# Two projections of the convolution branch computed by tokens in blocks of seven products, and the copies for the weight sums of w_out made earlier

## The chip, the cores and the metric

The kernel runs on one core of one Trainium2 chip. A time is the device time of one execution in microseconds (us); the time of a kernel is the median of its runs. The profile is of one more execution, and its times count from the first to the last instruction. In it PE is TensorE (matmuls; PEld is its weight load), DVE VectorE, ACT ScalarE, POOL GpSimd, SP the engine that issues most of the DMAs.

## The reference, cut to what matters

One layer over x of 256 tokens and 2048 channels, all in float32:

```python
hn = _rmsnorm(h, norm_w[i])
proj = hn @ w_in[i]                       # 2048 x 18432
q, v, f_fwd, f_bwd, z_a, b_gate, c_gate, h_b, z_b = jnp.split(proj, IN_SPLITS, axis=-1)
o_a = _hgrn2_bidirectional(jax.nn.silu(q), v, f_fwd, f_bwd, lb_all[:, i])
o_a = _head_rmsnorm(o_a, hgrn_norm_w[i]) * jax.nn.silu(z_a)
y_b = b_gate * _short_conv(c_gate * h_b, conv_w[i])      # width 3, per channel, along tokens
o_b = _rmsnorm(y_b, conv_norm_w[i]) * jax.nn.silu(z_b)
h = h + jnp.concatenate([o_a, o_b], axis=-1) @ w_out[i]  # 4096 x 2048
gate = jax.nn.sigmoid(h @ w_ple_gate[i])
h = h + (p[i] @ w_ple[i]) * gate
return _rmsnorm(h, final_norm_w)
```

Each of the nine groups of columns of w_in is 2048 wide. c_gate and h_b are needed only as their product, which the convolution then takes along the tokens, channel by channel.

## The kernel before, in words

**Products.** Every float32 value is split into a high and a low part; a float32 product is three matmuls (high by high, high by low, low by high). The weights come from HBM as blocks of 1 MB into `raw` (three buffers); `Stream` splits each half of a block (1024 columns) into `spl` (five buffers): ACT writes the high part (L121), DVE subtracts it for the low part (L122). Three splits are asked for ahead of use.

**Three ways to multiply.** `gemm_in` puts channels on the partitions: for a k-tile and 128 channels one 512-wide matmul (L427) and one 256-wide (L425); 32 such pairs make 256 channels of one projection, and `evac` adds the two parts (ACT L487, DVE L488). `gemm_vz` puts tokens on the partitions and takes v and z_a of two values of i at a time: `half` walks over eight blocks of two k-tiles, each as 24 products of 512 columns (3 per `three`, L547 to L549). A block named in `VZ_SUMS` takes seven block products in the place of eight, 21 instead of 24; for it `add_up` makes three sums of weights on DVE (L83), and the sums of x stand ready in `xq`. The result is scaled by the row norm afterwards. The output projection uses `half` too, with sums of mixa and mixb (L532 to L543) and sums of w_out that are prepared in DRAM: `prepare` copies 2 x 512 KB from DRAM to DRAM on SP's queue (L330), and `add_up` adds onto the copies by accumulating DMAs on POOL's queue (L338, L342).

**Stages.** Group A (`two_pairs`, i = 0, 2, 4, 6): q, forget gates, v and z_a, and the recurrence of two pairs of heads. Group B (loop at L924, i = 0 to 7, 256 channels each): c_gate, h_b, b_gate, z_b with `gemm_in`; the norm multiply of c_gate and the product with h_b on POOL; the convolution on DVE; y = convolution times b_gate on POOL; sigmoid of z_b on ACT; DVE's gate (L956), POOL's product (L960), and the split into mixb (ACT L973, DVE L974). In the same steps sums of mixa and mixb for the output are made. `pump` issues one of 48 accumulation steps after each POOL multiply and, after the last step of a sum, asks for the prepare of the fourth next one. Then come the output projection, the gate and the last norm.

**Order.** Functions write instructions; `at(dt, fn)` puts one off by dt ticks of the matmul loops; a priority scheduler sets the order on each engine, each of which runs its instructions in that order.

Of the kernel before, what the change touches and what calls it, by code (L numbers as in the profile page):

```python
# [8 lines left out]
F32 = mybir.dt.float32  # L9
# [128 lines left out]
def tile_hymba_encoder(  # L138
# [35 lines left out]
    VZ_ORDER, VZ_SUMS, VZ_OWN = range(8), (2, 4, 6), (2, 4, 6)  # L174
    dramp = ctx.enter_context(tc.tile_pool(name="dramp", bufs=1, space=bass.MemoryType.DRAM))
    vz_prepared = {}
    blocks = {}
    for i in range(0, 8, 2):
        for ii in (i, i + 1):
            for c in (B_FF, B_FB, B_Q):  # L180
                blocks[c, ii] = sum((ws.add(w_in[c + ii, h]) for h in range(2)), [])

        if i:
            blocks[B_V, i], vz_prepared[i] = [], []
            for q in VZ_ORDER:
                srcs = [
                    [w_in[c + i + b, q // 4, :, 2 * (q % 4) : 2 * (q % 4) + 2] for b in range(2)] for c in (B_V, B_ZA)
                ]
                if q in VZ_OWN:
                    blocks[B_V, i].append(ws.add_own(*srcs))  # L190
                elif q in VZ_SUMS:
                    sums = dramp.tile([P, 4, 512], F32, name=f"vz{i}_{q}")
                    vz_prepared[i].append((srcs, sums))
                    blocks[B_V, i].append(ws.add_sums(*srcs, sums))
                else:
                    blocks[B_V, i].append(ws.add(*srcs[0], *srcs[1]))
            continue
        for c in (B_V, B_ZA):
            blocks[c, i] = sum(
                (ws.add(*(w_in[c + i + b, q // 2, :, 4 * (q % 2) : 4 * (q % 2) + 4] for b in range(2))) for q in range(4)), []  # L200
            )
    for i in range(8):
        for c in (B_CG, B_HB, B_BG, B_ZB):
            blocks[c, i] = sum((ws.add(w_in[c + i, h]) for h in range(2)), [])
    first_out = len(ws.todo)
# [29 lines left out]
    rx, rb, rf, most, dummy = (few[:, 2 * j : 2 * j + 2] for j in range(5))  # L235
# [83 lines left out]
    now = [0]  # L319

    def at(dt, fn):
        pend.append((now[0] + dt, len(pend), fn))
# [69 lines left out]
    def x_norms():  # L392
        dve.tensor_reduce(out=rx, in_=ss8, op=ALU.add, axis=AX.X)
        act.activation(rx, rx, AF.Sqrt, bias=epst, scale=1.0 / D)
        dve.reciprocal(out=rx, in_=rx)
        for m in range(2):
            dve.tensor_copy(rw[m], rx[:, m : m + 1].broadcast_to([P, P]))
# [56 lines left out]
    xq = []  # L454

    def gemm_vz(i, vt, zt):

        acc = [psg.tile([P, 512], F32, tag="g", name=f"avz{i}_{b}") for b in range(4)]
        sc = [t.rearrange("p a b -> p (a b)") for t in scps]

        def extra():
            x, y = (psm.tile([P, 512], F32, tag=t, name=f"e{t}{i}") for t in "xy")
            return [x, y, *sc]

        main = [[acc[m], acc[2 + m]] for m in range(2)]
        for q1, q5, q6, q7 in half(main, extra, VZ_ORDER, VZ_SUMS, blocks[B_V, i], xs, xq[0], True):
            d = xq[1][:, 0]
            with tc.high_priority(offset=400):
                act.copy(out=vt[:, 0], in_=q1)
                dve.tensor_tensor(out=d, in0=vt[:, 0], in1=q6, op=ALU.subtract)  # L470
                dve.tensor_tensor(out=zt[:, 0], in0=q5, in1=d, op=ALU.subtract)
                dve.tensor_tensor(out=vt[:, 1], in0=d, in1=q7, op=ALU.subtract)
                dve.tensor_tensor(out=zt[:, 1], in0=zt[:, 0], in1=q7, op=ALU.add)
        with tc.high_priority(offset=400):
            for n, dst in enumerate((vt, zt)):
                for m in range(2):
                    dve.tensor_tensor(out=dst[:, m], in0=main[m][n], in1=dst[:, m], op=ALU.add)
            for dst in (vt, zt):
                for m in range(2):
                    act.activation(dst[:, m], dst[:, m], AF.Copy, scale=rx[:, m : m + 1])  # L480
# [36 lines left out]
    mixa = mixp.tile([P, NH * 2 * T + 8], F32R, name="mixa")[:, : NH * 2 * T]  # L517
    mixa = mixa.rearrange("p (k s t) -> p k s t", k=NH, s=2)
# [31 lines left out]

    def half(main, extra, order, which, parts, src, sums, every):
# [9 lines left out]
        for q, ids in zip(order, parts):  # L561
            k = 2 * q
            if len(ids) == 2:
                some_n = ((0,), (1,)) if every and q in (order[0], order[-1]) else ((0, 1),)
                for kk, n in ((kk, n) for ns in some_n for kk in range(2) for n in ns):
                    w = ws.get(ids[kk])[:, 0].rearrange("p s (b n) -> p b s n", b=2)
                    for m in range(2):
                        ah, al = (src[:, k + kk, s, m * P : (m + 1) * P] for s in range(2))
# [10 lines left out]
            def one(kk, m):  # L579
                return [src[:, k + kk, s, m * P : (m + 1) * P] for s in (1, 0)]  # L580

            def some(o):
                return [src[:, k, s, P:] if o == sums.shape[2] else sums[:, z, o, s] for s in (1, 0)]
# [228 lines left out]
    def two_pairs(i):  # L812
# [5 lines left out]
        if i == 6:  # L818
            for z in range(4):
                at(10 + 10 * z, lambda z=z: prepare(prepared[z]))  # L820
        else:


            todo = vz_prepared[i + 2]
            for z, what in enumerate(todo):
                at(50 + 10 * z, lambda what=what: prepare(what))
                for step in range(3):

                    dt = (166, 196, 220)[step] + z if i else 98 + 6 * step + z
                    at(dt, lambda what=what, step=step: add_up(what, step))  # L830
        if i == 2:

            def xsums(z):
                k = 2 * VZ_SUMS[z]
                a, t = xq[1][:, 0].rearrange("p (k t) -> p k t", k=2), xq[1][:, 1].rearrange("p (o t) -> p o t", o=4)
                act_sums(xs[:, k : k + 2], a, t, tc.keep_in_program_order)
                act_split(xq[0][:, z], xs[:, k : k + 2], t)
# [31 lines left out]
        if i == 0:  # L869
# [9 lines left out]
            xq.append(xqp.tile([P, len(VZ_SUMS), 4, 2, P], F32R, name="xsum"))  # L879
            xq.append(xqp.tile([P, 2, 512], F32, name="xd"))  # L880
# [10 lines left out]
        def rest():  # L891
# [5 lines left out]
            else:  # L897

                def keep():
                    kept.extend(psm.tile([P, 2, 2, P], F32, tag=f"sc{e}", name=f"kept{e}") for e in range(2))  # L900
                    finish_two(ogs, ss, zt, kept)
# [14 lines left out]
    mixb = None  # L916
# [6 lines left out]
    pool.memset(ysum, 0.0)  # L923
    for i in range(8):  # L924
        cg = ctmp.tile([P, 2, T], F32, tag="cg", name=f"cg{i}", bufs=2)
        evac(gemm_in(B_CG, i, TURNED if i % 2 == 0 else {}), lambda m: cg[:, m, :], ctmp)
        hb = ctmp.tile([P, 2, T], F32, tag="hb", name=f"hb{i}", bufs=2)
        evac(gemm_in(B_HB, i, {} if i else TURNED), lambda m: hb[:, m, :], ctmp)
        u = ub[i % 2]
        by_norms(cg, rbc2, 2)  # L930
        pump()
        pool.tensor_tensor(out=u[:, :, 1 : T + 1], in0=cg, in1=hb, op=ALU.mult)
        pump()
# [8 lines left out]
        evac(gemm_in(B_BG, i, {} if i else TURNED), lambda m: hb[:, m, :], ctmp)  # L942
# [6 lines left out]
        evac(gemm_in(B_ZB, i, TURNED if i in (0, 6) else {}), lambda m: hb[:, m, :], ctmp)  # L949
# [12 lines left out]
        if i == 0:  # L962
# [3 lines left out]
            mixb = bp.tile([P, NH, 2, T], F32R, name="mixb")  # L966
            og = bp.tile([P, 2, 2, 2, P], F32, name="og")
            suma = bp.tile([P, len(SUMS), 3, 2, P], F32R, name="suma")
        if i == 2:
            for e in range(2):  # L970
                act.copy(out=og[:, e], in_=kept[e])
        hi, lo = mixb[:, 2 * i : 2 * i + 2, 0, :], mixb[:, 2 * i : 2 * i + 2, 1, :]
        act.copy(out=hi, in_=cg)  # L973
        dve.tensor_tensor(out=lo, in0=cg, in1=hi, op=ALU.subtract)  # L974
        for src, z, n in ((mixa, i - 1, len(SUMS)), (mixb, i - SUMS[0], len(sumb32))):
            if 0 <= z < n:
                k = 2 * SUMS[z]
                a = ctmp.tile([P, 2, T], F32, tag="tmp", name=f"sa{i}")
                if src is mixb:
                    act_sums(mixb[:, k : k + 2], a, sumb32[z])  # L980
# [34 lines left out]
    tmp = spare.tile([P, 2, 512], F32, name="tmp")  # L1015
    tmps = [*(tmp[:, b] for b in range(2)), *(og[:, e].rearrange("p m h t -> p (m h t)") for e in range(2))]
# [46 lines left out]
    for u in range(2):  # L1063
# [9 lines left out]
        for src, sums, main, other, scale in ((mixa, suma, psg, psm, False), (mixb, sumb, psm, psg, True)):  # L1073
# [3 lines left out]
            if u == 0 and not scale:  # L1077
                for z in range(len(SUMS)):
                    k = 2 * SUMS[z]
                    if z == len(sumb32):  # L1080
                        sumb32.append(tmp[:, 0].rearrange("p (o t) -> p o t", o=4))
                        act_sums(mixb[:, k : k + 2], tmp[:, 1].rearrange("p (k t) -> p k t", k=2), sumb32[z])
                    act_split(sumb[:, z], mixb[:, k : k + 2], sumb32[z])
# [182 lines left out]
```

## Time and profile before

| | |
|---|---|
| median of 3 runs | 1111.88 us (1110.82 to 1114.4) |
| profiled execution | 1112.2 us |
| its span, first to last instruction | 1110.5 us |
| granted TensorE clock | 0.998 |
| group B | about 513 to 835 us of the span |
| v and z_a of a later pair in A | for example 195 to 239 us |

A row of a group reads: line, engine, operation, written tile <- read tiles, shape, count, busy time in all, mean ns of one, idle time before it and what ended that. A row of a timeline reads: start, duration, engine, line, and in brackets the idle time ahead of it and its releaser. Durations overlap where an engine works on instructions one behind the other.

### The profile page before, as it was taken

How to read it: one execution, taken by the hardware profiler on the slowest of the kernel's cores; microseconds unless marked ns; L12 is line 12 of the kernel's file. 1: busy time of each engine (PE TensorE's matmuls, PEld its weight loads, DVE VectorE, ACT ScalarE, POOL GpSimd, SP SyncE). 2: the span in 40 equal slices, each digit the busy share in tenths (PEclk: the TensorE clock that was granted, in tenths of full speed). 3: DMA queues.
4: the chain of work that ended last, by engine and by line, in shares of the span. 5: the costliest groups of instructions: out<-in, count | busy, mean ns of one | idle time of the engine just before them, and what ended most of it. 6: DMA issues, size and time to landing. Idle time of an engine off the chain costs nothing.

```text
span 1110.5 us, 16882 instructions
## 1 busy us (share of the span) xinstructions
PE 1100.5 (99%) x6455; PEld 945.7 (85%) x6455; DVE 851.4 (77%) x1127; ACT 677.3 (61%) x946; POOL 269.1 (24%) x215
## 2 busy tenths in 40 slices
PE   9999999999999999999999999999999999999997
PEld 8888888888888888888888888888888888888886
DVE  7799578896889778997657758856667888887673
ACT  6786577667876697575545535535546575575562
POOL 1045015203530325043334223424331000000101
PEclk9999999999999999999999999999999999999999
DMA  9755454564457744758999998999979887887542
GB/s 340 272 187 190 153 190 157 171 242 153 161 162 258 292 152 152 231 172 228 298 310 250 270 334 231 282 345 254 288 196 306 318 299 286 286 312 253 193 133 76
DMA packets 69808, 260.44 MB, mean 235 GB/s; under 512 B 7008, under 2 KB 16608, under 8 KB 52192
## 3 DMA queue, kind: packets, MB, share of 16 engines
q1 hardware_dynamic: 60480, 242.25, 62.1%
q0 software_dynamic: 8960, 16.78, 10.0%
q8 instruction: 51, 0.84, 0.3%
q10 hardware_dynamic: 288, 0.34, 0.1%
q14 instruction: 29, 0.24, 0.1%
HBM read 257.25 MB, written 35.65 MB: 264 GB/s over the span
## 4 chain that ended last, share of the span: by engine, by line
PE 98%; DMA 1%; ACT 0%; SPq 0%; DVE 0%; DVEq 0%; issue 0%; ACTq 0%
PE a L427 37%; PE a L425 19%; PE avz L547 3%; PE avz L548 3%; PE avz L549 3%; PE pg L1027 3%; PE pg L1026 3%; PE pg L1028 3%; PE pa L547 2%; PE pa L548 2%; PE pa L549 2%; PE a L446 1%; PE a L448 1%; PE a L447 1%; PE pb_sc L548 1%; PE pb_sc L549 1%
## 5 line engine op out<-in xcount | busy, mean ns | idle before, releaser
L122 DVE TENSOR_TENSOR spl<-raw,spl 128x1024 fp32r<-128x1024 f32 (+2 forms) x419 | 505.0, 1219 | 163.6 <-ACT spl L121 160.2
L427 PE MATMUL a<-xs,spl 128*128 128x512 f32 x1792 | 617.3, 395 | 0.6 <-ACT spl L121 0.6
L121 ACT CAST spl<-raw 128x1024 fp32r<-128x1024 f32 (+2 forms) x419 | 414.1, 999 | 255.0 <-PE a L425 81.9
L425 PE MATMUL a<-xs,spl 128*128 128x256 f32 x1792 | 483.8, 278 | 0.0
L427 PEld LDWEIGHTS a<-xs,spl 128*128 128x128 f32 x1792 | 332.2, 188 | 73.6 <-ACT spl L121 1.0
L425 PEld LDWEIGHTS a<-xs,spl 128*128 128x128 f32 x1792 | 334.6, 188 | 5.8 <-DVE spl L122 0.5
L1143 POOL TENSOR_TENSOR hh<-hh,fw 128x512 f32<-128x512 f32 (+1 forms) x9 | 11.0, 1227 | 250.7 <-ACT gt L1142 248.0
L487 ACT COPY r<-a 128x256 f32<-128x256 f32 x112 | 40.5, 368 | 37.3 <-PE a L425 35.8
L547 PE MATMUL avz<-spl,xs 128*128 128x512 f32 x138 | 54.0, 391 | 0.0
L549 PE MATMUL avz<-spl,xs 128*128 128x512 f32 x138 | 53.7, 389 | 0.0
L548 PE MATMUL avz<-spl,xs 128*128 128x512 f32 x138 | 53.7, 389 | 0.0
L1026 PE MATMUL pg<-spl,ht 128*128 128x512 f32 (+1 forms) x120 | 45.2, 377 | 0.0
L1027 PE MATMUL pg<-spl,ht 128*128 128x512 f32 (+1 forms) x120 | 45.1, 376 | 0.0
L1028 PE MATMUL pg<-spl,ht 128*128 128x512 f32 (+1 forms) x120 | 45.0, 375 | 0.0
L716 POOL TENSOR_TENSOR qc<-pf,ge 128x256 f32<-128x256 f32 x16 | 18.3, 1148 | 105.8 <-ACT dd L706 91.8
L492 POOL TENSOR_TENSOR xf<-xf,rbc 128x1024 f32<-128x1024 f32 x8 | 19.9, 2486 | 94.0 <-DVE rbc L403 50.2
L121 ACT CAST spl<-early 128x1024 fp32r<-128x1024 f32 (+1 forms) x29 | 28.7, 990 | 19.1 <-PE pb_y L549 7.5
L122 DVE TENSOR_TENSOR spl<-early,spl 128x1024 fp32r<-128x1024 f32 (+1 forms) x29 | 32.9, 1147 | 9.2 <-ACT spl L121 8.8
L547 PE MATMUL pa<-spl,mixa 128*128 128x512 f32 x88 | 34.5, 392 | 0.0
L549 PE MATMUL pa<-spl,mixa 128*128 128x512 f32 x88 | 34.3, 389 | 0.0
L548 PE MATMUL pa<-spl,mixa 128*128 128x512 f32 x88 | 34.2, 389 | 0.0
L716 POOL TENSOR_TENSOR kc<-dd,ge 128x256 f32<-128x256 f32 x16 | 27.7, 1728 | 19.8 <-DVE dd L707 13.6
(321 smaller groups left out, 1641.7 us busy)
## 6 DMA issues: line engine op xcount, KB each, us to landing
raw<-in_w_in_dram SPq DMA_DIRECT2D x106, 1024.0 KB, 6.9
raw<-in_w_in_dram SPq DMA_DIRECT2D x100, 256.0 KB, 3.9
raw<-in_w_out_dram SPq DMA_DIRECT2D x36, 512.0 KB, 5.2
sums<-in_w_out_dram SPq DMA_DIRECT2D x32, 512.0 KB, 10.6
raw<-in_w_in_dram SPq DMA_DIRECT2D x26, 512.0 KB, 5.2
raw<-sums SPq DMA_DIRECT2D x13, 1024.0 KB, 5.3
raw<-in_w_gate_dram SPq DMA_DIRECT2D x9, 1024.0 KB, 5.1
sums<-in_w_out_dram POOLq DMA_DIRECT2D x16, 512.0 KB, 10.1
```

Source lines behind the costliest of these rows:

```text
L121: self.nc.scalar.copy(out=v[:, :, 0], in_=r)
L122: self.nc.vector.tensor_tensor(out=v[:, :, 1], in0=r, in1=v[:, :, 0], op=ALU.subtract)
L425: pe.matmul(a[:, :T], lhsT=lhsT, rhs=xs[:, kt, 0, :], start=False, stop=(kt == NKT - 1))
L427: pe.matmul(a, lhsT=lhsT, rhs=xs[:, kt, :, :].rearrange("p s n -> p (s n)"), start=(kt == 0), stop=False)
L487: act.copy(out=r, in_=acc[m][:, 1, :])
L547: pe.matmul(acc, lhsT=ah, rhs=w[:, 0], start=start, stop=False)
L548: pe.matmul(acc, lhsT=ah, rhs=w[:, 1], start=False, stop=False)
L549: pe.matmul(acc, lhsT=al, rhs=w[:, 0], start=False, stop=stop)
L716: pool.tensor_tensor(out=c64(dst[:, d]), in0=c64(src[:, d, :, half * P : (half + 1) * P]), in1=g.unsqueeze(3).broadcast_to([P, 2, 2, CH]), ...
L1026: pe.matmul(acc[m], lhsT=lh, rhs=wh, start=(kt == 0), stop=False)
L1027: pe.matmul(acc[m], lhsT=lh, rhs=wl, start=False, stop=False)
L1028: pe.matmul(acc[m], lhsT=ll, rhs=wh, start=False, stop=(kt == nk - 1))
```

## The change

For i = 2, 4 and 6, c_gate and h_b of two values of i are computed together, tokens on the partitions, by `gemm_pair`, which is taken out of `gemm_vz`. Blocks 2 and 4 of eight are done as seven products. The results a and b become a * rx2 * b (rx2 is the square of the row norm) by two DVE instructions, are transposed by PE (eight 128x128 transposes) at 12 ticks into the b_gate projection, and ACT copies them to the convolution's input. POOL's norm multiply and product are gone for these i.

The sums of x for blocks 2 and 4 have to live through group B and move to the end of `mixa`; mixb becomes eight tiles, the last two of which share their place with a and b. The kept results of A go to another SBUF tile in the place of PSUM.

The prepares of w_out's sums are no longer asked for by `pump`: each of the four stages of A issues four of them. Four of the accumulation steps are asked for within each new stage.

```diff
-    for i in range(8):
+    CH_SUMS = (2, 4)
+    for i in range(2):
         for c in (B_CG, B_HB, B_BG, B_ZB):
             blocks[c, i] = sum((ws.add(w_in[c + i, h]) for h in range(2)), [])
+    for i in range(2, 8, 2):
+        blocks[B_CG, i] = []
+        for q in VZ_ORDER:
+            srcs = [
+                [w_in[c + i + b, q // 4, :, 2 * (q % 4) : 2 * (q % 4) + 2] for b in range(2)] for c in (B_CG, B_HB)
+            ]
+            blocks[B_CG, i].append(ws.add_own(*srcs) if q in CH_SUMS else ws.add(*srcs[0], *srcs[1]))
...
         if steps_up:
             n, step = steps_up.pop(0)
             add_up(prepared[n], step)
-            if step == 2 and n + 4 < len(prepared):
-                prepare(prepared[n + 4])
...
-        if i == 6:
-            for z in range(4):
-                at(10 + 10 * z, lambda z=z: prepare(prepared[z]))
...
+        for z in range(4):
+            at(10 + 22 * z, lambda z=z: prepare(prepared[2 * i + z]))
...
-            xq.append(xqp.tile([P, len(VZ_SUMS), 4, 2, P], F32R, name="xsum"))
-            xq.append(xqp.tile([P, 2, 512], F32, name="xd"))
+            xq.extend((late[:, 0], late[:, 1], xqp.tile([P, 4, 2, P], F32R, name="xsum")))
+            xd.append(xqp.tile([P, 2, 512], F32, name="xd"))
...
+    def convolved(i, ut):
+
+        for ii in (i, i + 1):
+            tp = psm.tile([P, 2, T], F32, tag="xy"[ii % 2], name=f"ut{ii}")
+            for h in range(2):
+                c = (2 * (ii % 2) + h) * P
+                for m in range(2):
+                    pe.transpose(tp[:, h, m * P : (m + 1) * P], ut[:, m, c : c + P], ident)
+            act.copy(out=ub[ii % 2][:, :, 1 : T + 1], in_=tp)
+
+    def gemm_ch(i):
+
+        def get():
+            a, b = (bp.tile([P, 2, 512], F32, tag=f"late{e}", name=f"ch{i}_{e}") for e in range(2))
+            return a, b, early[:, 0:512]
+
+        for z in range(4):
+            at(5 + 10 * z, pump)
+        a, b = gemm_pair(f"ch{i}", CH_SUMS, blocks[B_CG, i], get)
+        with tc.high_priority(offset=300):
+            for m in range(2):
+                dve.scalar_tensor_tensor(
+                    out=a[:, m], in0=a[:, m], scalar=rx2[:, m : m + 1], in1=b[:, m], op0=ALU.mult, op1=ALU.mult
+                )
+        at(12, lambda: convolved(i, a))
+
     for i in range(8):
...
-        evac(gemm_in(B_ZB, i, TURNED if i in (0, 6) else {}), lambda m: hb[:, m, :], ctmp)
+        hb = ctmp.tile([P, 2, T], F32, tag="hb", name=f"zb{i}", bufs=2)
+        evac(gemm_in(B_ZB, i, kick), lambda m: hb[:, m, :], ctmp, 500 if i in (1, 3, 5) else 200)
```

What `gemm_pair` does behind its products is what `gemm_vz` did; line numbers move by up to some 40 (L122 and L83 stay; L427 becomes L433, L425 L431, L488 L500, L956 L997, L960 L1001, L974 L1017, L532 L545, L535 L548).

On DVE, where the stage for i = 4 begins: the first seven-product block's weights are `raw_6323`; they get three sums (L83) and four splits (L122), among which the gate of i = 3 (L997), mixb's low part (L1017) and the sums of mixa and mixb (L545, L548) stand.

```order
669 L83 TENSOR_TENSOR raw_6323<-raw_6323 128x2x512
670 L997 SCALAR_TENSOR_TENSOR zb_6188<-zb_6188,vec,szb_6285 128x256
671 L545 TENSOR_TENSOR sa_6293<-mixa 128x512
672 L122 TENSOR_TENSOR spl_6350<-raw_6323,spl_6350 128x512
673 L1017 TENSOR_TENSOR mixb_5141<-cg_6175,mixb_5141 128x2x256
674 L83 TENSOR_TENSOR raw_6323<-raw_6323 128x512
675 L122 TENSOR_TENSOR spl_6365<-raw_6323,spl_6365 128x2x512
676 L83 TENSOR_TENSOR raw_6323<-raw_6323 128x512
677 L548 TENSOR_TENSOR sb_6294<-sa_6293 128x128 x2
678 L548 TENSOR_TENSOR sb_6294<-sa_6293,sb_6294 128x128 x2
679 L545 TENSOR_TENSOR sa_6304<-mixb_5141 128x512
680 L122 TENSOR_TENSOR spl_6386<-raw_6323,spl_6386 128x2x512
```

The same place before, where c_gate of i = 4 begins:

```order
660 L122 TENSOR_TENSOR spl_6362<-raw_6341,spl_6362 128x4x256
661 L956 SCALAR_TENSOR_TENSOR hb_6003<-hb_6003,vec,szb_6292 128x256 x2
662 L532 TENSOR_TENSOR sa_6302<-mixa 128x512
663 L535 TENSOR_TENSOR sb_6303<-sa_6302 128x128
664 L122 TENSOR_TENSOR spl_6383<-raw_6381,spl_6383 128x4x256
665 L974 TENSOR_TENSOR mixb<-cg_5914,mixb 128x2x256
666 L535 TENSOR_TENSOR sb_6303<-sa_6302 128x128
667 L535 TENSOR_TENSOR sb_6303<-sa_6302,sb_6303 128x128 x2
668 L532 TENSOR_TENSOR sa_6313<-mixb 128x512
669 L122 TENSOR_TENSOR spl_6411<-raw_6381,spl_6411 128x4x256
```

Behind the first gate row two splits stood before (664, 669); now three splits (672, 675, 680) and two sums of weights (674, 676) of one block stand there, with the third sum (669) right ahead, in line with the same gate and mix rows.

On POOL, from the gate product of i = 1 (L1001, before L960) to the product of the convolution and b_gate of i = 2 (L983, before L943), in the change:

```order
125 L1001 TENSOR_TENSOR cg_5146<-cg_5146,zb_5429 128x512
126 L349 DMA sums_0_5_84<-sums_0_5_84 128x512
127 L345 DMA sums_1_2_85<-in_w_out_dram 256x1x512
128 L345 DMA sums_1_3_86<-in_w_out_dram 256x1x512
129 L345 DMA sums_1_4_87<-in_w_out_dram 256x1x512
130 L345 DMA sums_1_5_88<-in_w_out_dram 256x1x512
131 L983 TENSOR_TENSOR cg_5955<-cg_5955,bg_5854 128x512
```

And before:

```order
125 L960 TENSOR_TENSOR cg_5116<-cg_5116,hb_5205 128x512
126 L342 DMA sums_0_5_84<-sums_0_5_84 128x512
127 L492 TENSOR_TENSOR cg_5515<-cg_5515,early 128x512
128 L338 DMA sums_1_2_85<-in_w_out_dram 256x1x512
129 L932 TENSOR_TENSOR ub_4596<-cg_5515,hb_5604 128x2x256
130 L338 DMA sums_1_3_86<-in_w_out_dram 256x1x512
131 L943 TENSOR_TENSOR cg_5515<-cg_5515,hb_5604 128x512
132 L338 DMA sums_1_4_87<-in_w_out_dram 256x1x512
```

The multiplies that stood between the accumulating copies are gone, so that four stand one behind the other.

More of the change, by code (lines that the diff above doesn't have):

```diff
@@ L201, in tile_hymba_encoder @@
             )
-    for i in range(8):
+    CH_SUMS = (2, 4)
+    for i in range(2):
         for c in (B_CG, B_HB, B_BG, B_ZB):
             blocks[c, i] = sum((ws.add(w_in[c + i, h]) for h in range(2)), [])
+    for i in range(2, 8, 2):
[6 more added lines that the diff above has]
+        for ii in (i, i + 1):
+            for c in (B_BG, B_ZB):
+                blocks[c, ii] = sum((ws.add(w_in[c + ii, h]) for h in range(2)), [])
     first_out = len(ws.todo)
@@ L234, in tile_hymba_encoder @@
     few = const.tile([P, 16], F32, name="few")
-    rx, rb, rf, most, dummy = (few[:, 2 * j : 2 * j + 2] for j in range(5))
+    rx, rb, rf, most, dummy, rx2 = (few[:, 2 * j : 2 * j + 2] for j in range(6))
     xf32 = xp.tile([P, NKT, T], F32, name="xf32")
@@ L395, in x_norms @@
         dve.reciprocal(out=rx, in_=rx)
+        dve.tensor_tensor(out=rx2, in0=rx, in1=rx, op=ALU.mult)
         for m in range(2):
@@ L477, in gemm_vz @@
                     dve.tensor_tensor(out=dst[:, m], in0=main[m][n], in1=dst[:, m], op=ALU.add)
+        return vt, zt
+    def gemm_vz(i, vt, zt):
+        gemm_pair(f"vz{i}", VZ_SUMS, blocks[B_V, i], lambda: (vt, zt, xd[0][:, 0]))
+        with tc.high_priority(offset=400):
             for dst in (vt, zt):
@@ L1072, in tile_hymba_encoder @@
             )
-        for src, sums, main, other, scale in ((mixa, suma, psg, psm, False), (mixb, sumb, psm, psg, True)):
+        for src, sums, main, other, scale in ((mixa, sums_a, psg, psm, False), (mixb, sums_b, psm, psg, True)):
             name = f"p{'ab'[scale]}{u}"
```

91 lines of the change are left out of this document (47 added, 44 removed).

## The prediction

> **What bounds the kernel now.** I read first the spans, then the chain of waits, then what TensorE (PE) waited for.
>
> ```profile
> span 1110.5 us, 16882 instructions
> PE 1100.5 (99%) x6455; PEld 945.7 (85%) x6455; DVE 851.4 (77%) x1127; ACT 677.3 (61%) x946; POOL 269.1 (24%) x215
> PE 98%; DMA 1%; ACT 0%; SPq 0%; DVE 0%; DVEq 0%; issue 0%; ACTq 0%
> core 0: 1110.5 us, clock 0.998
> PE wps L266 <- DVE wz L261: 1.1, 1, 1.1
> PE a L427 <- ACT spl L121: 0.6, 1, 0.6
> ```
>
> The chain is 98% matmuls, the granted clock is 0.998, and the last two rows are the whole list of PE's waits: 1.7 us, both at the start. So nothing but less matmul work makes this kernel shorter, and any weight split that comes late makes it longer at once. DVE, at 77%, has time over on average; whether it has in one stage must be asked there. The next rows are stretches of the span; their columns are the stretch, its length, busy time of PE, weight loads, DVE, ACT and POOL with counts, clock, DMA share and GB/s.
>
> ```profile
> 568.40:612.80 44.40, 44.40 (x258) 38.83 (x257) 28.83 (x40) 21.06 (x30) 17.82 (x12) 1.00 0.94 257
> 330.30:352.06 21.76, 21.76 (x98) 18.02 (x97) 19.44 (x21) 12.87 (x14) 0.00 (x0) 1.00 0.69 221
> 195.00:239.00 44.00, 44.00 (x273) 36.51 (x273) 40.20 (x45) 27.74 (x34) 5.63 (x4) 1.00 0.61 202
> 474.00:513.00 39.00, 39.00 (x313) 34.55 (x312) 34.84 (x43) 22.97 (x44) 16.72 (x13) 1.00 0.67 198
> 513.00:835.00 322.00, 322.00 (x1860) 281.59 (x1859) 216.84 (x293) 156.87 (x215) 109.38 (x89) 1.00 0.93 274
> 251.70:262.91 11.21, 11.21 (x66) 9.62 (x64) 8.45 (x10) 6.90 (x17) 5.58 (x5) 1.00 0.49 182
> ```
>
> The first is four projections with channels on the partitions in group B: 128 pairs of a 512-wide and a 256-wide matmul. The second is 96 token-major 512-wide products. The third is a whole v/z_a stage, where blocks of seven products are already in use: DVE has 40.20 of 44.00 us to do there and PE still lost nothing. The fifth is group B, with DMA at 0.93.
>
> **The change part by part.**
>
> *Matmuls.* Per pair of i (three pairs) four projections of 32 matmul pairs go. I price them at 44.39 us (11.09 each; the window's 44.40 less its cut edges). In their place come eight blocks, six of 24 products and two of 21: 186 products. From the second window one is 21.76 / 96 = 0.2267 us, so 42.17 us. Added are eight transposes per pair; their price stands in the chain, where eight of the same shape lie between two projection matmuls:
>
> ```profile
> 182.73 0.23 PE a L427
> 182.97 0.12 PE a L425
> 183.09 0.87 PE ogt L658 x8
> 183.96 0.23 PE a L427
> L658 PE MATMUL ogt<-ident,ogz x24: 270/272/273, 182.9 to 418.5; 128*128 128x128 f32 x24
> ```
>
> 0.87 us, and I add 0.09 for two groups of four going in separately, and 0.06 for the moved kicks of the weight order. Per pair 42.17 + 0.87 + 0.15 - 44.39 = -1.2; three pairs give **-3.6 us**. As PE waited for nothing in B, this is also the most that can be gained.
>
> The Trainium skill, "TensorE: Matmul & The Clock Gate", Part 4 (PE-mode transpose), gives some 275 ns for one 128x128 transpose inside a kernel, with the PE's access latency as its largest part. Twenty-four of them one behind the other would be an estimated 6.6 us and leave no gain. The last row above agrees with that figure as a duration (272 ns), but the chain row shows that the next one starts after 0.87 / 8 = 0.109 us, so the trace goes with the overlap.
>
> *DVE, in the new stage.* The elementwise cost is where a stall can come from. Rows from the same work in B now (start, duration, instruction):
>
> ```profile
> 600.21 2.35 DVE L122 TENSOR_TENSOR spl<-raw,spl 128x1024 fp32r<-128x1024 f32 x2
> 615.31 0.42 DVE L488 TENSOR_TENSOR hb<-a,r 128x256 f32<-128x256 f32 x1
> 618.17 0.87 DVE L956 SCALAR_TENSOR_TENSOR hb<-hb,vec,szb 128x256 f32<-128x256 f32 x2
> 619.08 0.69 DVE L532 TENSOR_TENSOR sa<-mixa 128x512 f32<-128x512 f32 x1
> 619.80 1.27 DVE L535 TENSOR_TENSOR sb<-sa 128x128 f32<-128x128 f32 x1
> 622.13 0.68 DVE L974 TENSOR_TENSOR mixb<-cg,mixb 128x512 fp32r<-128x512 f32 x1
> 617.20 0.63 ACT L953 ACTIVATE szb<-hb 128x512 f32<-128x512 f32 x1 [0.28 <-POOL hb L492]
> 620.96 0.62 ACT L973 CAST mixb<-cg 128x512 fp32r<-128x512 f32 x1 [1.27 <-POOL cg L960]
> 615.87 1.29 POOL L492 TENSOR_TENSOR hb<-hb,rbc 128x512 f32<-128x512 f32 x1 [6.44 <-DVE hb L488]
> 619.19 1.74 POOL L960 TENSOR_TENSOR cg<-cg,hb 128x512 f32<-128x512 f32 x1 [1.24 <-DVE hb L956]
> L83 DVE TENSOR_TENSOR raw<-raw 128x512 f32<-128x512 f32 x6 | 4.6, 763 | 0.2
> L83 DVE TENSOR_TENSOR raw<-raw 128x1024 f32<-128x1024 f32 x3 | 3.7, 1217 | 0.0
> L122 DVE TENSOR_TENSOR spl<-raw,spl 128x1024 fp32r<-128x1024 f32 x18 | 22.8, 1282 | 3.0 <-ACT spl L121 2.6
> ```
>
> Of two 1024-wide splits in a dense row the second starts 1.14 us after the first (2.35 for both, with the last one's tail); I take that for the 1024-wide weight sum too, and 0.6 for a 512-wide one, about half. The last three rows, of the third window's stage, are means of busy time, 1.28, 1.22 and 0.76: longer, since instructions behind one another overlap.
>
> The tight place is the first seven-product block. PE reaches its last summed weights after 48 products of blocks 0 and 1 and 21 of its own: 69 x 0.2267 = 15.64 us after the stage's start. In that time DVE has, by the order shown for the pair that starts at i = 4 (the excerpt has the last twelve rows): the evacuation of the projection before (0.84), three wide splits (3.42) and a narrow one (0.66), three weight sums (2.3), the two gates (0.86), two 512-wide sums of mixa and mixb (1.44), the four small ones (1.06), mixb's low part (0.68): 11.3 us. The rest is waiting: the sums of weights stand in line behind the gate L997, and this behind POOL's 1.29 and ACT's 0.63; the mixb rows stand behind POOL's 1.74 and ACT's 0.62; the evacuation ends only 1.7 us in. Walking these rows one by one, each starting when its releaser is done, the last split is ready 15.7 to 15.8 us after the start against 15.64. At i = 2, without the mixb sum, it is ready at 15.1 to 15.3, and at i = 6 earlier. So I put **+0.2 us** on the path, all at i = 4. The lower bound is 0, the upper, with the means of busy time in the place of the distances, 2.3 + 4.8 = 7.1 us. I take the low one: the v/z_a stage above works with these same blocks at 91% DVE and no wait.
>
> *POOL.* The norm multiply of c_gate and the product with h_b go from POOL for six of the eight i; it is at 24%, so this is worth nothing by itself. The result goes out by ACT's copy from PSUM instead; the next conv needs it during the b_gate projection, 11 us, and takes two copies of some 0.6 us. Nothing on PE waits there.
>
> *Copies of w_out.* Twelve pairs of copies move from B into the first three stages of A. They run beside PE; what they can delay is a raw load. Rows for the queues (share of all 16 engines) and for issue to landing:
>
> ```profile
> q1 hardware_dynamic: 60480, 242.25, 62.1%
> q0 software_dynamic: 8960, 16.78, 10.0%
> sums<-in_w_out_dram SPq DMA_DIRECT2D x32, 512.0 KB, 10.6
> raw<-in_w_in_dram SPq DMA_DIRECT2D x106, 1024.0 KB, 6.9
> 573.52 1.05 ACT L121 CAST spl<-raw 128x1024 fp32r<-128x1024 f32 x1 [4.81 <-DMA raw<-in_w_in_dram]
> ```
>
> In the last stage of A four such pairs already run, and the fourth window shows PE full there at a DMA share of 0.67. I take **0** for them, since 22 ticks apart they are spread wider than these; if that cover is gone, one late load at the stage with the narrowest lead would cost up to its 6.9 us less the 5.5 us that two splits cover, so 0 to +1.4. B loses the same bytes: its 0.93 falls, and the split that waited 4.81 us for a load (and cost PE nothing) has more room. Worth 0 too, as no PE wait stands behind it.
>
> **Sum.** The profiled execution took 1112.2 us, 0.3 above the median of 1111.88. 1112.2 - 3.6 + 0.2 = 1108.8 for a profiled one, **1108.5** for the median. A difference under 0.3% (3.3 us) can't be told from none in a measurement of this kernel; the forecast lies at that edge.
>
> **The rivals.**
>
> *A: DVE is late for the seven-product blocks.* Place: first sum block at i = 2 and 4. For it: DVE there has gate, mix sums and weight sums in one line in program order, and one late POOL multiply (rows of POOL in B reach far more than 1.74) moves the whole line:
>
> ```profile
> 576.31 2.14 POOL L492 TENSOR_TENSOR hb<-hb,rbc 128x512 f32<-128x512 f32 x1 [10.88 <-DVE hb L488]
> 588.22 4.48 POOL L492 TENSOR_TENSOR cg<-cg,early 128x512 f32<-128x512 f32 x1 [5.54 <-DVE cg L488]
> ```
>
> Against it: the third window. By the means of busy time it costs 7.1: 1112.2 - 3.6 + 7.1 - 0.3 = 1115.4, slower. It decides the sign from 1.2 us of stall per pair.
>
> *B: four accumulations at once.* The four 512 KB accumulating copies that were spread between POOL's multiplies now stand back to back in each new stage. By q0's row 16.78 MB cost 10.0% of 1110.5 us, 111 us of all engines; so 2 MB are 13.9. At even turns the burst lasts 27.8 us, in which the loads get half of the engines and need 0.61 (third window): they fall 0.11 x 27.8 = 3.1 us behind. Two buffers of one block each ahead are 48 x 0.2267 = 10.9 us, against 6.9 for a load to land: room 4.0, and no stall. If the burst goes wholly first, loads are 0.61 x 13.9 = 8.5 us late; less the room and less the one split that lies ready (12 x 0.2267 = 2.7) PE loses 1.8 per pair: 1108.5 + 5.4 = 1113.9. For it: stages of B where single splits wait for a load exist already. Against it: they cost PE nothing at a DMA share of 0.93, and the new stage has the prepares' bytes less.
>
> *C: the saved time is lost to a slower pace.* Projections that follow products run slower at first: the last window has 32 pairs at 11.21 in A against 11.09 in B. With that for the four projections behind each new stage, 3 x 4 x 0.12 = +1.4: 1109.9.
>
> *D: the transposes don't overlap* as the three groups of eight in A do, since each four wait for their own PSUM bank: 24 x 0.27 - 2.6 = +3.9, thus 1112.4. Against it: the chain row.
>
> **Chances.** Forecast 0.55 (0.38 faster, 0.17 within). A 0.16 (0.12 slower, 0.04 within), B 0.09 (0.03 and 0.06), C 0.14 (0.04 faster, 0.10 within), D 0.06 (within). Faster 0.42, same 0.43, slower 0.15. The forecast's own range is 1107.5 to 1110. With A and B the range goes up to 1115, which leaves out half of A; down it goes to 1106.5, since beyond the 3.6 only the scatter of a median (1.1 below it in the three runs) can help.
>
> **What would show it.** PE rows in the three new stages: 186 products in 42.2 us and no wait on a split; any wait at the first sum block with ACT or DVE splits as releaser is A, with a raw load as releaser B. The eight transposes in the chain at about 0.9 us; 2 us would be D. The projections behind at 11.1; 11.2 is C. DVE above 0.9 in the new stages, B's DMA share well under 0.93 and the first stages of A with more. The prediction is wrong if PE waits more than 1.2 us in a new stage, or anywhere in A.

## The result, and the profile after

The changed kernel is slower: 1125.33 us (1123.09 to 1126.57, 4 runs) against 1112.2, a ratio of 1.0114 with the interval 1.0091 to 1.0137. The forecast was 1108.5, in a range up to 1115. The profiled execution took 1123.09, its span is 10.9 us longer than that of before. The page of the changed kernel, then the whole list of what PE waited for:

```profile
span 1121.4 us, 16647 instructions
PE 1102.3 (98%) x6269; PEld 939.9 (84%) x6269; DVE 889.1 (79%) x1164; ACT 684.9 (61%) x943; POOL 246.9 (22%) x203
PE 90%; DMA 4%; DVE 3%; ACT 2%; SPq 1%; POOL 0%; issue 0%; DVEq 0%; ACTq 0%; POOLq 0%
PE ach L560 <- ACT spl L121: 7.0, 3, 2.7
PE ach L561 <- DVE spl L122: 2.3, 3, 0.8
PE wps L272 <- DVE wz L267: 1.1, 1, 1.1
```

186 matmuls fewer, and yet a longer span: the chain is matmuls for 90% only, and DMA, which had 1%, now has 4%. The first two rows of waits are new: three waits of up to 2.7 us for a high part and three of up to 0.8 us for the low part of the same split, one of each in every new stage (`ach` are the new stage's products). The three new stages, and then what PE did right behind the waits (columns as before; the clock is the last but two):

```profile
566.96:614.52 47.56, 44.33 (x188) 36.00 (x187) 36.46 (x44) 22.17 (x27) 8.80 (x8) 0.96 0.88 237
659.84:708.92 49.08, 45.63 (x188) 36.91 (x187) 37.88 (x50) 22.61 (x28) 8.80 (x8) 0.93 0.91 240
754.26:799.65 45.39, 42.75 (x189) 34.84 (x188) 34.19 (x37) 21.92 (x25) 8.64 (x8) 1.00 0.94 256
595.43:600.85 5.42, 4.65 (x12) 3.51 (x13) 3.99 (x4) 3.38 (x5) 0.00 (x0) 0.69 0.96 344
688.57:695.54 6.97, 6.21 (x14) 4.64 (x15) 5.71 (x6) 5.03 (x6) 0.00 (x0) 0.54 0.93 349
```

Where 42.17 was forecast stand 47.56, 49.08 and 45.39: 15.5 us too much in three stages, more than four times the 3.6 us that the matmuls save. Not all of it is waiting: in the first two stages the granted clock falls to 0.69 and 0.54 behind the wait. The chain at the first of the three, in order of time (start, duration, what):

```profile
579.16 1.23 DVE spl L122
580.41 0.34 SPq L100
580.80 0.54 SPq L100
581.38 0.71 SPq L100
582.13 12.10 DMA raw<-in_w_in_dram
594.34 1.05 ACT spl L121
595.41 1.24 DVE spl L122
596.70 0.53 PE ach L561
597.22 0.43 PE ach L562
```

The split of 579.16 is the last of block 2, the first seven-product block. It frees the load buffer, and the load of block 5 goes out in four pieces. The last of them takes 12.10 us to land, and PE has run out of work since 592.8. (The last row is a product behind the waits: 0.43 us to the next one where 0.23 is usual.) What lay on the DMA engines meanwhile (queue: packets, MB, share of the 16 engines; then issues):

```profile
q0 software_dynamic: 1210, 2.32, 77.7%
q1 hardware_dynamic: 729, 1.34, 20.6%
raw<-in_w_in_dram SPq DMA_DIRECT2D x11, 256.0 KB, 10.9
sums<-in_w_out_dram POOLq DMA_DIRECT2D x4, 512.0 KB, 14.6
```

This is the stretch from 574.75 to 594.25 us. q0 carries the four accumulating copies of 512 KB that stand back to back on POOL, q1 all loads. Over the whole stretch the copies hold 78% of the engines and the loads 21%. That is not yet what a load gets beside the copies, since for about half of this time no packet of a load moves at all. The first row below is the whole of the queues from the issue at 580.41 to 584 us; the other two are the stretch from 585 to 593 us, in which both queues have packets all the time:

```profile
q0 software_dynamic: 278, 0.54, 100.5%
q0 software_dynamic: 543, 1.05, 70.6%
q1 hardware_dynamic: 548, 1.01, 38.4%
```

So the load of block 5 loses time twice. It moves nothing for more than 3.5 us after its issue. Then the two queues move packet for packet (543 and 548), but a packet of a copy holds its engine for 0.706 x 16 x 8 us / 543 = 0.17 us and one of a load for 0.384 x 16 x 8 / 548 = 0.09 us, so that the loads have 38% of the engines and move 0.13 MB per us. (Packets overlap a little; the shares add up to 109%.)

### The profile page after: what moved, and what is told of

Same layout as the page of the kernel before. It is cut to its first block, busy times and chain, and to the rows that moved or that the text cites. A ratio compares the mean times of both kernels' runs of the same rounds, so it can differ in the third digit from the quotient of the medians.

```text
span 1121.4 us, 16647 instructions
## 1 busy us (share of the span) xinstructions
PE 1102.3 (98%) x6269; PEld 939.9 (84%) x6269; DVE 889.1 (79%) x1164; ACT 684.9 (61%) x943; POOL 246.9 (22%) x203
## 4 chain that ended last, share of the span: by engine, by line
PE 90%; DMA 4%; DVE 3%; ACT 2%; SPq 1%; POOL 0%; issue 0%; DVEq 0%; ACTq 0%; POOLq 0%
PE a L433 29%; PE a L431 15%; DMA raw<-in_w_in_dram 3%; PE avz L560 3%; PE avz L562 3%; PE avz L561 3%; PE pg L1071 3%; PE pg L1072 3%; PE pg L1070 3%; PE ach L561 2%; PE ach L562 2%; PE ach L560 2%; DVE spl L122 1%; PE pa L561 1%; PE pa L562 1%; PE pa L560 1%
## 5 line engine op out<-in xcount | busy, mean ns | idle before, releaser
L122 DVE TENSOR_TENSOR spl<-raw,spl 128x1024 fp32r<-128x1024 f32 (+2 forms) x431 | 518.1, 1217 | 148.9 <-ACT spl L121 145.1
L121 ACT CAST spl<-raw 128x1024 fp32r<-128x1024 f32 (+2 forms) x431 | 423.4, 994 | 282.6 <-PE a L431 69.1
L433 PE MATMUL a<-xs,spl 128*128 128x512 f32 x1408 | 483.8, 395 | 0.0
L431 PE MATMUL a<-xs,spl 128*128 128x256 f32 x1408 | 376.6, 278 | 0.0
L433 PEld LDWEIGHTS a<-xs,spl 128*128 128x128 f32 x1408 | 259.9, 188 | 55.3
L431 PEld LDWEIGHTS a<-xs,spl 128*128 128x128 f32 x1408 | 262.5, 188 | 5.6
L560 PE MATMUL ach<-spl,xs 128*128 128x512 f32 x156 | 62.7, 402 | 7.0 <-ACT spl L121 7.0
L561 PE MATMUL ach<-spl,xs 128*128 128x512 f32 x156 | 62.8, 403 | 2.3 <-DVE spl L122 2.3
L562 PE MATMUL ach<-spl,xs 128*128 128x512 f32 x156 | 62.6, 401 | 0.0
L983 POOL TENSOR_TENSOR cg<-cg,bg 128x512 f32<-128x512 f32 x8 | 11.2, 1406 | 189.6 <-DVE bg L500 189.6
L499 ACT COPY r<-a 128x256 f32<-128x256 f32 x88 | 31.5, 368 | 31.8 <-PE a L431 31.7
L560 PEld LDWEIGHTS ach<-spl,xs 128*128 128x128 f32 x156 | 30.4, 195 | 14.7 <-ACT spl L121 8.3
L83 DVE TENSOR_TENSOR raw<-raw 128x512 f32<-128x512 f32 (+1 forms) x45 | 41.2, 915 | 0.8
L122 DVE TENSOR_TENSOR spl<-early,spl 128x1024 fp32r<-128x1024 f32 (+1 forms) x29 | 32.9, 1147 | 9.3 <-ACT spl L121 8.7
```

Of the source, the lines that this page charges most:

```text
L83: self.nc.vector.tensor_tensor(out=out, in0=out, in1=other, op=ALU.add)
L121: self.nc.scalar.copy(out=v[:, :, 0], in_=r)
L122: self.nc.vector.tensor_tensor(out=v[:, :, 1], in0=r, in1=v[:, :, 0], op=ALU.subtract)
L431: pe.matmul(a[:, :T], lhsT=lhsT, rhs=xs[:, kt, 0, :], start=False, stop=(kt == NKT - 1))
L433: pe.matmul(a, lhsT=lhsT, rhs=xs[:, kt, :, :].rearrange("p s n -> p (s n)"), start=(kt == 0), stop=False)
L499: act.copy(out=r, in_=acc[m][:, 1, :])
```

## The experiments

My theory after the trace: the four accumulating copies, asked for in one go, take the DMA engines from the new stage's loads, whose rows are short. Its rivals: the seven-product block itself (DVE's sums, a buffer kept long); the burst alone, whatever stands beside it; the copies of w_out moved to group A.

**The burst taken out of the stage.** In the loop the four steps were put behind the multiplies of b_gate and z_b:

```diff
-        for z in range(4):
-            at(5 + 10 * z, pump)
...
         pool.tensor_tensor(out=cg, in0=cg, in1=hb, op=ALU.mult)
         pump()
+        if i >= 2:
+            pump()
...
         by_norms(hb, rbc, 2)
         pump()
+        if i >= 2:
+            pump()
```

> The change, but with no accumulating copy asked for inside the three new stages: each of those twelve steps of 512 KB goes out behind a POOL multiply of the b_gate and z_b stages. If the four copies in a row are what makes the load of block 3 late (12 us to land), PE has no wait in the new stages, its clock stays up, and the time is the changed kernel's less some 15 us of stall and slow clock that its trace shows: 1107 to 1111. If instead the seven-product block itself is late on DVE, or holds its load buffer too long, 2 us or more of wait per stage stay and the time stays at 1120 to 1126.

Measured: 1115.01 us (10 runs), ratio 1.0025 (1.0016 to 1.0035). 10 us of the loss are gone, but not all. The stage at i = 2 takes 42.17 us, to the hundredth what the sum said; the one at i = 4 46.03, the one at i = 6 42.88. At i = 4 (the first two rows are PE's waits in the whole run, then the chain, then ACT's row):

```profile
PE ach L560 <- DVE zb L500: 1.6, 2, 1.2
PE ach L561 <- DVE spl L122: 1.3, 2, 1.1
634.09 14.45 DMA raw<-in_w_in_dram
648.63 1.05 ACT L121 CAST spl<-raw 128x1024 fp32r<-128x1024 f32 x1 [4.90 <-DMA raw<-in_w_in_dram]
```

The four copies went out between 625.5 and 636.3 us now, and met the first loads of the next new stage, which are asked for some 20 us ahead: 14.45 us to land. DVE takes its rows in order, so the evacuation behind the late split was late too, and PE waited for its PSUM (the first row). The copies had been moved, not spread.

**The burst alone, in the kernel before.**

```diff
+        early_four = i in (2, 4, 6)
+        for _ in range(4 if early_four else 0):
+            pump()
         cg = ctmp.tile([P, 2, T], F32, tag="cg", name=f"cg{i}", bufs=2)
...
         by_norms(cg, rbc2, 2)
-        pump()
+        if not early_four:
+            pump()
```

(the same at the next three multiplies)

> The kernel before, with its twelve accumulating copies of 512 KB put into the same bursts of four that the change makes, at the same place (right behind the gate product of i = 1, 3 and 5). The loads next to them are here 1 MB in rows of 8 KB. If the burst alone is enough, PE waits some 3 us in each of the three places and the time goes to about 1122. If it also needs the new stage's loads in rows of 2 KB (loads and accumulating copies take turns by packets, so that small packets get less of the engines), the loads land in 8 to 9 us, PE waits for nothing or under 1 us in all, and the time is 1111 to 1114.

Measured: 1118.5 us, ratio 1.0056 (1.004 to 1.0071), between the two forecasts: the burst alone costs half of the loss. Here the loads are 1 MB in rows of 8 KB; the 20 us from the start of the first burst:

```profile
q0 software_dynamic: 973, 1.86, 63.8%
q1 hardware_dynamic: 399, 2.97, 36.9%
raw<-in_w_in_dram SPq DMA_DIRECT2D x3, 1024.0 KB, 11.3
sums<-in_w_out_dram POOLq DMA_DIRECT2D x4, 512.0 KB, 18.8
```

One packet of the loads carries 2.97 MB / 399 = 7.4 KB; in the changed kernel it was 1.34 / 729 = 1.8 KB, in the copies it is 1.9 in both. Until 586 us only one packet of a load moves, so this stretch too is read better where both queues have packets all the time, from 590 to 600 us:

```profile
q1 hardware_dynamic: 362, 2.67, 66.4%
q0 software_dynamic: 371, 0.73, 39.1%
```

The turns are packet for packet here as well (362 and 371), but now a load's packet is the longer one: the loads have 66% of the engines and move 0.27 MB per us, twice what they move in the changed kernel.

**Only one seven-product block.**

```diff
-    CH_SUMS = (2, 4)
+    CH_SUMS = (4,)
...
-        for q1, q5, q6, q7 in half(main, extra, VZ_ORDER, sums_of, ids, xs, xq, True):
+        for q1, q5, q6, q7 in half(main, extra, VZ_ORDER, sums_of, ids, xs, xq[VZ_SUMS.index(sums_of[0]) :], True):
```

> The change, but only block 4 of the new stages as seven products, block 2 as eight: the burst meets regular blocks alone. Three products of 0.2267 us more per stage, 2.0 us in all, when nothing else changes. If the seven-product block at this place is the cause (DVE's sums late, its buffer kept long), the waits at block 3 go and the time is 1110 to 1113. If the burst is the cause, the load of block 3 still lands 12 us after its issue, is needed 0.7 us later than before, and the waits shrink by little: 1120 to 1126.

Measured: 1113.43 us (10 runs), ratio 1.0012 (1.0002 to 1.0021). My expectation was wrong: I had put the late load at block 3, and thought that the seven products matter by 0.7 us only. The late load is that of block 5, in the buffer that block 2 gives back. As a seven-product block it gives it back at 580.41, after its three sums and last split; as a regular one at 576.12:

```profile
576.12 0.34 SPq L100
578.97 13.57 DMA raw<-in_w_in_dram
PE ach L561 <- DVE spl L122: 2.2, 3, 0.8
```

The load takes as long or longer (13.57 us), lands 1.7 us earlier at 592.5, and PE wants it 0.7 us later. What is left is the short wait for the low part, 0.8 us at most, with no drop of the clock. So both are needed for most of the loss: the burst makes the load slow, and the seven-product block makes it start 4.3 us late.

**The copies of w_out alone, in the kernel before.** As in the change: four prepares in each stage of A, none from `pump`.

```diff
-            if step == 2 and n + 4 < len(prepared):
-                prepare(prepared[n + 4])
...
+        for z in range(4):
+            at(10 + 22 * z, lambda z=z: prepare(prepared[2 * i + z]))
```

> The kernel before, with only the copies of w_out moved: four in each stage of group A, none from the accumulation steps in B. If that part is hidden as I took it, the time is that of the kernel before (1110 to 1114) and PE waits for nothing in A; if it costs, a wait on a split with a raw load as releaser shows in the first three stages of A.

Measured: 1111.33 us (10 runs), ratio 0.9992 (0.9983 to 1.0002): no change, as taken, and no wait of PE in A.

**No accumulating copies behind i = 1.**

```diff
-    steps_up = [(4 * g + n, step) for g in range(len(prepared) // 4) for step in range(3) for n in range(4)]
+    steps_up = [(4 * g + n, step) for g in range(1) for step in range(3) for n in range(4)]
...
-        for z in range(4):
-            at(5 + 10 * z, pump)
```

> The change with the accumulating copies of the last three of four groups left out, so that none runs after i = 1 (the sums of w_out of these groups are then not sums, and the output projection works with wrong weights; all other work is done). If the accumulating copies alone turn the gain into a loss, PE waits for nothing in the new stages, each takes 42.2 us, and the time is what the sum of matmuls said: 1108 to 1109.5. If DVE is late at i = 4 by itself, as one rival of the prediction has it, 1 us or more of wait stays there, and the time is 1110 or more.

Measured: 1107.89 us, ratio 0.9964 (0.995 to 0.9978). The new stages at i = 4 and 6, and the loads from 574 to 594 us:

```profile
654.95:697.15 42.20, 42.20 (x188) 34.91 (x187) 37.71 (x50) 22.26 (x28) 3.03 (x2) 1.00 0.60 203
742.48:784.67 42.19, 42.19 (x188) 34.93 (x187) 34.37 (x37) 21.97 (x25) 2.90 (x2) 1.00 0.60 201
raw<-in_w_in_dram SPq DMA_DIRECT2D x12, 256.0 KB, 3.9
q1 hardware_dynamic: 955, 1.75, 88.4%
```

The same pieces land in 3.9 us, not 10.9. The last row is q1 from 582 to 588 us: without copies beside them the loads move 0.29 MB per us, and the first packets of the load issued at 580.91 move before 582. And the stages take what the sum of products said. DVE has 37.71 of 42.20 us to do at i = 4, and costs nothing. With that, the seven products, the transposes and DVE's line are off the list as causes by themselves: without the later copies there is no loss. (That the seven-product block adds to what the copies do was shown by the run with only one such block.)

**The copies moved to A.** All work done; 28 of 48 steps in A, in another order of the steps:

```diff
+    turns = [(0, 0)]
+    for g in range(1, 4):
+        turns += [(g - 1, 1), (g, 0), (g - 1, 2)]
+    turns += [(3, 1), (3, 2)]
+    steps_up = [(4 * g + n, step) for g, step in turns for n in range(4)]
...
+        for z in range((0, 4, 12, 12)[i // 2]):
+            at(20 + 16 * z if i == 2 else 12 + 8 * z, pump)
```

> The change with its accumulating copies moved: of the 48 steps 28 go out in group A, where the loads of its projections have rows of 8 KB, 12 at i = 0 and 1, and 8 of 256 KB at i = 2 and 4 behind the multiplies of b_gate and z_b; none in a new stage, and the next step of a sum follows eight others. If the accumulating copies beside the new stages' loads are the whole loss, the gain comes out: 1107.5 to 1110, below the kernel before. If they cost as much wherever they are put, waits on late loads show in A and the time is 1112 or more.

Measured: 1114.84 us (8 runs), ratio 1.0026 (1.0015 to 1.0036). The new stages take 42.17 to 42.19 us, but A now loses (PE's wait, then POOL in the stage of i = 4):

```profile
PE avz L564 <- DVE qt L504: 4.1, 3, 1.9
305.69 3.17 POOL L345 DMA_DIRECT2D sums<-in_w_out_dram  x3
307.39 4.00 POOL L349 DMA_DIRECT2D sums<-sums  x3
308.99 4.82 POOL L508 TENSOR_TENSOR xf<-xf,rbc 128x1024 f32<-128x1024 f32 x1
```

Six issues stood ahead of POOL's multiply L508, which ended some 6 us late; ACT's next split stood behind its result, and the evacuation of q behind that split on DVE. This is not a late load: it is the time that POOL needs to issue, in front of a row that others wait for. By the chain of this run POOL is done with the six issues at 311.39, 5.7 us after the first began, and the multiply takes 2.43 us from there.

**Rows of 2 KB, with and without the burst, in the kernel before.**

```diff
+            if j in self.fine:
+                for k in range(0, 8, 2):
+                    self.nc.sync.dma_start(dst[:, b, k : k + 2], src[:, k : k + 2])
```

(for c_gate and h_b of i = 2 to 7)

> The kernel before with the bursts of four (as in the run that moved these alone, 1118.5) and with the loads of c_gate and h_b of i = 2 to 7 issued as four pieces with rows of 2 KB instead of one with 8 KB; bytes, buffers and all engine work are the same. If the size of the rows decides what the loads get beside the accumulating copies, a load takes 12 us and more in the bursts and the time goes to 1123 to 1132. If the rows do not matter it stays at 1117 to 1120.

> The kernel before with only these loads in rows of 2 KB, its accumulating copies spread as they were. If small rows cost nothing without a burst: 1111 to 1113. If the loads lose to single accumulating copies too, waits of 1 us and more show and the time is 1114 to 1120.

Measured: with the burst 1124.95 us, ratio 1.0107 (1.0074 to 1.0141); without it 1115.18, ratio 1.0031 (1.0017 to 1.0044). Short rows cost 3 us by themselves beside the copies as they were, and 6.5 beside bursts (1124.95 - 1118.5). The edit also makes four issues of one, and the two are not told apart. The longest waits with the burst (the first row: 5.6 us in two waits, the longer 3.4) stand just ahead of a burst, though, not behind it: there loads in pieces take 11.7 us, beside the prepares, which are still in B in this kernel, and single steps (the other rows, 640 to 668 us):

```profile
PE a L433 <- ACT spl L125: 5.6, 2, 3.4
q1 hardware_dynamic: 2774, 7.10, 80.4%
q0 software_dynamic: 416, 0.77, 19.6%
raw<-in_w_in_dram SPq DMA_DIRECT2D x13, 256.0 KB, 11.7
sums<-in_w_out_dram SPq DMA_DIRECT2D x4, 512.0 KB, 7.9
```

So that loads in short rows cost is shown; that it is the burst that makes them cost here is not.

**The copies placed.** From the run that moved them to A: the steps only where POOL had been idle for 6 to 13 us, none ahead of L508, and in B none at odd i from 3 on and none in a new stage.

```diff
+        for dt in ((), range(38, 46, 2), range(12, 28, 4), range(12, 28, 4))[i // 2]:
+            at(dt, pump)
+        if i >= 4:
+            for dt in range(38, 46, 2):
+                at(dt, pump)
...
+    turns = [(0, 0), (0, 1), (1, 0), (1, 1), (2, 0)]
+    turns += [(0, 2), (3, 0), (2, 1)]
+    turns += [(1, 2), (3, 1), (2, 2), (3, 2)]
```

> The change with all its work and other places for the accumulating copies, chosen by the run that moved them to A and lost 4 us to POOL: there six copies stood ahead of a POOL multiply that the first projection products of the v/z_a stage wait for. Now 20 steps go out in A, all where POOL waited for DVE for 6 to 13 us, none ahead of that multiply; 12 at i = 0 and 1; 16 of 256 KB at i = 2, 4 and 6 behind the multiplies of b_gate and z_b; none at odd i from 3 on and none in a new stage. If the loss is only where these copies run, PE waits for nothing in A and in the new stages and the time is 1107.5 to 1109.5. If four copies of 512 KB in a row cost PE beside loads of 8 KB rows as well, as the burst alone did in B (5 us for three), it is 1110 to 1114.

Measured: 1107.17 us (1107.14 to 1108.47), ratio 0.996 (0.9947 to 0.9974), with all the work done: faster than both kernels. Four copies of 512 KB stand in a row in A there too, and cost PE nothing. Its whole list of waits is the one at the start:

```profile
span 1105.4 us, 16636 instructions
PE wps L272 <- DVE wz L267: 1.1, 1, 1.1
```

**Two copies in the stage in the place of four.**

```diff
-        for z in range(4):
+        for z in range(2):
             at(5 + 10 * z, pump)
...
+        if i in (2, 4, 6):
+            pump()
```

(the last two lines twice, behind the multiplies of b_gate and z_b)

> The change with two of the four 512 KB copies in each new stage, and the other two behind the multiplies of b_gate and z_b of i = 2, 4 and 6; the rest as in the change. If the load of block 5 is late by what the copies take of the DMA engines, half of them make it land some 4 us sooner (the four held the engines 14 to 19 us), about when it is needed: waits of 0 to 1 us per stage, no drop of the clock, and 1109 to 1114. If any copy beside these loads is enough to make them late, the waits stay near 3 us and the time at 1120 or more.

Measured: 1110.0 us (10 runs), ratio 0.9981 (0.9971 to 0.9991). The pieces land in 8.4 us:

```profile
raw<-in_w_in_dram SPq DMA_DIRECT2D x12, 256.0 KB, 8.4
PE ach L561 <- DVE spl L122: 1.2, 3, 0.9
q0 software_dynamic: 76, 0.13, 14.9%
q1 hardware_dynamic: 906, 1.66, 88.1%
```

Two copies less are worth 15 us: landing goes from 10.9 to 8.4, and the waits from 9.3 us with slow clock to 1.2 without. The last two rows (585 to 590 us) show one reason why half of the copies cost so much less than half: two copies are nearly through when the load's packets begin, and soon leave the engines to it. The other is that the load has a time by which it is needed; only what it lands later than that costs PE.

## Why the prediction was wrong, step by step

*Matmuls, -3.6: right.* In the run without later copies a new stage takes 42.2 us (42.17 forecast); the four projections behind it with their transposes take 45.3, against 44.39 + 0.87 + 0.15 = 45.4; from the first of the eight transposes to the product behind them it is 0.79 us. The overlap of transposes is confirmed, and rival D falls. So does rival C, by which the four projections would have taken some 45.9.

*DVE, +0.2: right in size (0), and rival A falls.* DVE's line was late only as a consequence, where a load was late ahead of it (first experiment). The list of waits names splits of ACT and DVE, which the prediction had put down as the sign of A; but they stand at block 5 and not at the first sum block, and the chain shows that ACT's split itself waited for the load.

*Prepares in A, 0: right.*

*The accumulating copies: wrong.* They had no term in the sum, only rival B, at a chance of 0.09 and a price of 0 to 5.4 us. They cost 15.5 us in the changed kernel's trace. Three steps of B failed:

1. "At even turns ... the loads get half of the engines." The turns were even by packets, not by time. The packets are nearly of a size in the new stage (1.9 and 1.8 KB), but one of the copies held an engine for 0.17 us and one of the loads for 0.09: the loads got 38% of the engines and 0.13 MB per us, less than half of the 0.29 that they move without the copies. Before that, their first packet moved only 3.5 us and more after the issue, where it takes about 1 us without the copies; for this the step has no term. The Trainium skill, "DMA: Bandwidth & Descriptors", Queues, rings and completion order, has each engine alternate between queue rows by packets. The trace agrees in this, by the packets that the profile counts: 548 of the loads against 543 of the copies with 1.8 KB in one, 362 against 371 with 7.4 KB, where the loads' share of the time rose to 66%. I had worked in shares of time, and had priced the row size of the new loads nowhere, although the v/z_a stage already loads in such pieces of 256 KB.

2. "Room 4.0." I counted two whole blocks ahead of a landing. The load of block 5 can only go out when the seven-product block 2 has been split, 580.41 - 566.96 = 13.45 us into the stage; PE needs it after 114 products, 25.84 us in. Less 2.3 us for the split and 1.7 for the four issues that leaves 8.4 us for the last piece, which took 12.1. I had walked DVE's rows to see when the weights are ready, and not asked what the same late row frees.

3. "PE loses 1.8 per pair." Behind the waits at i = 2 and 4 the matmuls themselves run slower (0.69 and 0.54 of the clock, 427 ns from one to the next where 227 are usual), 8 of them at i = 2 and 13 at i = 4: 1.6 and 2.6 us more. From product to product, less the usual 0.23 us, the two waits of a stage, with one product between them, are 2.6 + 1.0 and 2.8 + 1.0 us there; at i = 6 they are 2.0 + 1.0, and the clock stayed full. The Trainium skill, "TensorE: Matmul & The Clock Gate", Part 1, has the gate watch windows of some 3.4 us, which run on their own; the trace fits this, with 3.1 us on the one side and 3.7 and 3.9 on the other, but three cases do not show it.

The three together: 3.7 + 3.9 + 3.1 us of waits beyond the usual distance, and 4.2 of slow clock, are 14.9 of the 15.5; the rest lies at the product right behind the second wait, with 0.33, 0.59 and 0.34 us to the next one where 0.23 is usual. What is left of the difference of spans (-3.6 + 15.5 = 11.9 against 10.9) lies ahead of the first v/z_a stage, which began 1.5 us earlier in this execution, and in 0.7 us more in the output stage.

What stays open: how much of the loss belongs to the row size and how much to the burst in the new stage itself. Both were shown to cost in the kernel before (3 and 6.5 us there), where loads, buffers and prepares lie otherwise. Open too is why the first packet of a load comes so late behind the burst.

## What to carry to other kernels

When a change makes work denser, look up every transfer whose place in its queue was set by the instructions that are taken away: here four accumulating copies had been held apart by POOL's multiplies, and fell together when these went. For each load in the new stage work out the time from the release of its buffer to its use, and compare it with its landing time beside the worst neighbour, not with a mean one; short rows get less beside another queue (0.13 MB per us here, against 0.27 with rows of 8 KB). And a gain is not lost for good by such a clash: with the copies at other places the same change gives 0.4%.

## What the runs showed that I had not expected

Four copies of 512 KB, 2 MB in all, kept 78% of sixteen DMA engines for 19.5 us, and a load of 256 KB pieces went from 3.9 to 10.9 us. Waits of 3.9 us in one stage cost 2.6 us more behind them by the clock. Two DMA queues took turns packet for packet, with rows of 2 KB and of 8 KB alike. Six DMA issues on POOL, which held it for 5.7 us ahead of one multiply, were enough to stop PE two engines away.
